# A hybrid decoder block: the causal mask added on VectorE, the latent norms' gains folded into the matrices, gates and output weights prepared in other places

## The chip, the core and the metric

The kernel runs on one core of one Trainium2 chip. A core has five engines that run side by side, each with its own queue: TensorE (PE, its weight loads PEld) for matrix products, VectorE (DVE) and ScalarE (ACT) for elementwise work, GpSimd (POOL), and SyncE (SP), which here only issues transfers. Products end in PSUM, everything else lies in SBUF. The metric is the time of one execution on the device in microseconds (us).

## What is computed

One decoder layer over 2048 tokens of width 1024, in fp32. Eight heads of attention with forget gates ("fox") and eight heads of latent attention ("mla") share an input projection; then come an output projection, a squared-ReLU MLP and a last norm. Cut to what the change touches:

```python
proj  = rmsnorm(x, attn_norm_g) @ w_in           # fq, fk, fv, f_logit, c_q, c_kv, k_rope
log_f = log_sigmoid(f_logit + b_forget)          # fox: decay, cumulated over the sequence
F     = cumsum(log_f)
c_q   = rmsnorm(proj[c_q],  q_norm_g)            # 384 wide
c_kv  = rmsnorm(proj[c_kv], kv_norm_g)           # 256 wide
k_rope = rope(proj[k_rope])
q  = c_q  @ w_uq                                 # 8 heads x (64 + 32 rotated)
kv = c_kv @ w_ukv                                # 8 heads x (64 keys + 64 values)
logits = scale * q @ k.T  (+ F_t - F_s for fox)
logits = where(key_pos <= q_pos, logits, -inf)   # causal
out = softmax(logits) @ v
mixed = concat(rmsnorm(fox, fox_out_g), rmsnorm(mla, mla_out_g))
x = x + mixed @ w_o
```

## The kernel before

Products run on fp32 values cut in two: `hi` is rounded to the format that TensorE takes at full rate, `lo` is the rest, and `mm3` (L138 to L140) makes the three products hi*hi, lo*hi, hi*lo. The cut itself is `split_ps` (from PSUM, ScalarE writes hi in L105, VectorE subtracts in L106) or `split_w` (from SBUF, L113 on GpSimd and L116 on VectorE).

The front part goes twice over 1024 tokens (pass 0 and pass 1). In each pass `latent` makes the 384 (c_q) and then the 256 + 32 + 8 columns (c_kv, rotary key, gate logit) of eight token tiles, two tiles at a time: product, copy out of PSUM, sum of squares on ScalarE (L413), the reciprocal root as six small operations on GpSimd (`rstd_pool`, L94 to L99), the scaling by root and gain on VectorE (L418), and, three steps later, the transposes (L424) and the split. `load_heads` cuts w_uq and w_ukv per group of heads. `mla_rows`, `mla_v` and `mla_qrope` multiply the latents with them and store queries, keys and values to DRAM. `rotary_keys` rotates the shared key (L496 to L499), `forget_gates` computes log sigmoid and its cumulated sum (L514 to L530, 32 operations on tiles of 128 columns, then two small products). `fox` makes the projections of the fox heads for the pass in 21 products (three of the c range, q, k and v, with seven each); while it runs, `ahead` prepares the next pass, in pass 0 the norms and transposes of the next tiles (`prep`, L350 and L355). The operand splits for fox are L589 (`split_operand`) and L609 (`fox_prep`). Work is put off by `later(n, ...)` and done by `flush`, and what is pinned (`keep_in_program_order`) stands on its engine where the program has it; the rest is placed by a scheduler.

The attention runs over units of four query tiles (a head of fox, then one of mla, two heads being one "head pair"). `score_steps` takes the keys of a query tile in chunks of up to 1024: score products into one of two buffers `ps_s` (L861), in the last chunk also the mask, as a product of a bf16 identity with a bf16 128x128 mask that is accumulated into the last 128 columns (L864); then the negated maximum on VectorE (L866), the exponential with its sum on ScalarE (L867), and a normalisation of the probabilities on GpSimd (L887) after a few 128x1 or 128x2 operations on VectorE (L875 to L884). Of 384 chunks 256 are a query tile's last. `value_steps` transposes the probabilities (L907), splits them (L105, L106), multiplies them with the values (L924, L925), and adds two halves on GpSimd after a transfer (L930, L935). All steps are laid on one list by numbers of ticks, each step at its due tick. `prepare_wo` (L950 to L952, GpSimd) multiplies the output weights by the gains and cuts them, four row blocks at a time, at two places near the end of the list.

The mask and the gain's place in the loop are these lines:

```python
if n == 0 and kb + wb == (t + 1) * P:
    nc.tensor.matmul(ps[:, i, wb - P:wb], identb, maskb, start=False, stop=False)
...
nc.vector.scalar_tensor_tensor(cn[:, b], cn[:, b], r[:, b:b + 1], gain, ALU.mult, ALU.mult)
```

## Time and profile before

| | |
|---|---|
| median of 3 runs | 2935.13 us (2934.0 to 2937.68) |
| profiled execution | 2932.08 us, its span 2930.3 us |
| PE busy | 2808.3 us, 96% |
| DVE busy | 2220.2 us, 76% |
| ACT busy | 1413.7 us, 48% |
| POOL busy | 1371.5 us, 47% |
| mean granted clock of TensorE | 0.986 |

Busy shares are of the span. The stages, in us from its start: latents of pass 0 to 112, keys and values to 150, fox of pass 0 to 263; the same for pass 1 to 350, 425 and 540; attention from 540 to 1470, whose steady part (640 to 1300) repeats every 110 us; output projection to 1640; the MLP to the end. Matmuls are pipelined, so the start-to-start step tells their cost, not the busy time of one. A wait is put down to the releaser that came last.

### The profile page before, as it was taken

To read this page: it belongs to the slowest core of one execution; us is meant where nothing else is said; L and a number is where in the kernel's file an instruction comes from. 1 tells how busy PE (TensorE), PEld (TensorE's weight loads), DVE (VectorE), ACT (ScalarE), POOL (GpSimd) and SP (SyncE) were. 2 spreads that over 40 slices of the span, in tenths; PEclk is the share of its full clock that TensorE was granted. 3 is DMA by queue.
4 is the path that set the end of the run, shared out by engine and by line. 5 is a ranking of instruction groups with operands and counts; after the bars stand their busy time and mean duration, and the time that the engine had idled before them with its cause. 6 is when DMAs were issued, how large, how long until landed. Compare 5 with 4: busy or idle time off the path is not lost. (4 is left out here: it accounts for less than half of the span.)

```text
span 2930.3 us, 40573 instructions
## 1 busy us (share of the span) xinstructions
PE 2808.3 (96%) x14634; PEld 2365.1 (81%) x14634; DVE 2220.2 (76%) x3089; ACT 1413.7 (48%) x2493; POOL 1371.5 (47%) x996
## 2 busy tenths in 40 slices
PE   8899979899999999999999899999999999999998
PEld 7789958788888888887778788888888788878886
DVE  7767486588888888888767755667666678897898
ACT  5244233487787787787533422233222433334432
POOL 2726453445545545547532355556556233453421
PEclk9999989999999999999999999999999999999999
DMA  5456434835335335332245564455445744455551
GB/s 155 160 197 190 152 133 160 236 76 121 77 93 121 76 93 121 76 93 62 69 164 208 208 208 151 143 216 223 151 158 190 269 151 148 157 212 175 199 194 58
DMA packets 262520, 442.95 MB, mean 151 GB/s; under 512 B 41712, under 2 KB 150384, under 8 KB 255600
## 3 DMA queue, kind: packets, MB, share of 16 engines
q1 hardware_dynamic: 206848, 300.75, 34.8%
q10 hardware_dynamic: 55472, 139.61, 12.4%
q8 instruction: 116, 1.90, 0.3%
q14 instruction: 84, 0.69, 0.1%
HBM read 275.54 MB, written 156.37 MB: 147 GB/s over the span
## 5 line engine op out<-in xcount | busy, mean ns | idle before, releaser
L1299 PE MATMUL mm<-big,mid 128*128 128x512 f32 x2688 | 615.9, 390 | 2.7 <-ACT big L1374 2.5
L1299 PEld LDWEIGHTS mm<-big,mid 128*128 128x128 f32 x2688 | 504.5, 188 | 112.7 <-ACT big L1374 7.2
L140 PE MATMUL mm<-big,mid 128*128 128x512 f32 x1312 | 513.9, 393 | 8.9 <-DVE mid L249 6.7
L861 PE MATMUL ps_s<-big,big 96*128 96x384 f32 (+11 forms) x1720 | 445.1, 379 | 5.3 <-ACT mid L867 5.0
L139 PE MATMUL mm<-big,big 128*128 128x512 f32 (+2 forms) x1160 | 436.5, 376 | 1.2 <-DVE big L249 1.2
L138 PE MATMUL mm<-big,big 128*128 128x512 f32 (+2 forms) x1072 | 403.5, 376 | 0.4 <-ACT big L248 0.4
L887 POOL TENSOR_SCALAR mid<-mid,rl,fac 128x768 f32<-128x768 f32 (+4 forms) x256 | 255.9, 1010 | 290.2 <-DVE rl L884 170.8
L866 DVE TENSOR_REDUCE negm<-ps_s 128x1 f32<-128x896 f32 (+7 forms) x384 | 348.2, 907 | 51.6 <-PE ps_s L861 47.5
L248 ACT ACTIVATE big<-mid 128x1024 fp32r<-128x1024 f32 (+1 forms) x222 | 218.3, 1046 | 322.4 <-PE mm L139 193.7
L255 POOL TENSOR_TENSOR mid<-mid,mid 128x1024 f32<-128x1024 f32 x88 | 241.2, 2741 | 262.2 <-DVE mid L249 112.6
L867 ACT ACTIVATE mid<-ps_s,negm 128x896 f32<-128x896 f32 (+7 forms) x384 | 332.5, 866 | 46.2 <-DVE negm L866 34.1
L907 PE MATMUL ps_t<-ident,mid 128*128 128x128 f32 x2176 | 339.8, 274 | 5.3 <-POOL mid L887 5.3
L907 PEld LDWEIGHTS ps_t<-ident,mid 128*128 128x128 f32 x2176 | 274.5, 141 | 59.1 <-POOL mid L887 5.9
L861 PEld LDWEIGHTS ps_s<-big,big 96*128 96x128 f32 (+2 forms) x1720 | 290.1, 193 | 22.2 <-ACT mid L867 9.6
L1210 POOL TENSOR_TENSOR mid<-mid,mid 128x1024 f32<-128x1024 f32 x60 | 198.8, 3340 | 232.0 <-DVE big L249 218.8
L140 PEld LDWEIGHTS mm<-big,mid 128*128 128x128 f32 x1312 | 248.1, 189 | 62.1 <-DVE mid L249 7.5
L249 DVE TENSOR_TENSOR mid<-mid,mid 128x1024 fp32r<-128x1024 f32 x112 | 193.3, 1754 | 117.4 <-ACT mid L248 83.4
L105 ACT ACTIVATE big<-ps_t 128x512 fp32r<-128x512 f32 (+3 forms) x427 | 225.0, 534 | 108.4 <-PE ps_t L907 101.0
L106 DVE TENSOR_TENSOR big<-ps_t,big 128x512 fp32r<-128x512 f32 (+3 forms) x427 | 254.2, 602 | 28.6 <-ACT big L105 25.0
L139 PEld LDWEIGHTS mm<-big,big 128*128 128x128 f32 x1160 | 220.4, 190 | 37.8 <-DVE big L249 2.0
L138 PEld LDWEIGHTS mm<-big,big 128*128 128x128 f32 x1072 | 203.8, 190 | 33.3 <-ACT big L248 1.1
L138 PE MATMUL mm<-big,mid 128*128 128x512 f32 x528 | 209.1, 397 | 12.3 <-DVE big L106 6.9
(225 smaller groups left out, 5151.9 us busy)
## 6 DMA issues: line engine op xcount, KB each, us to landing
gd<-mid ACTq DMA_DIRECT2D x109, 512.0 KB, 3.0
mid<-gd SPq DMA_DIRECT2D x109, 512.0 KB, 3.5
mid<-in_w_up SPq DMA_DIRECT2D x64, 512.0 KB, 5.2
mid<-in_w_down SPq DMA_DIRECT2D x64, 512.0 KB, 5.2
mid<-in_x SPq DMA_DIRECT2D x32, 512.0 KB, 5.8
xd<-mid ACTq DMA_DIRECT2D x28, 512.0 KB, 5.4
big<-xd SPq DMA_DIRECT2D x14, 1024.0 KB, 8.8
mid<-in_w_in SPq DMA_DIRECT2D x24, 512.0 KB, 4.0
```

Of the source, the lines that this page charges most:

```text
L105: nc.scalar.activation(hi, ps, AF.Copy)
L106: nc.vector.tensor_tensor(lo, ps, f32v(hi), ALU.subtract)
L138: nc.tensor.matmul(ps, lh, rh, start=(k == 0), stop=False)
L139: nc.tensor.matmul(ps, lh, rl, start=False, stop=False)
L140: nc.tensor.matmul(ps, ll, rh, start=False, stop=(k == nk - 1))
L255: (eng or nc.gpsimd).tensor_tensor(t, raws[a], raws[b], op)
L861: nc.tensor.matmul(ps[:, i, 0:wm], l[0:rows, qs], r[0:rows, kb:kb + wm], start=(n == 0), stop=(n == len(ops) - 1))
L866: nc.vector.tensor_reduce(negm[:, j, c:c + 1], src, AX.XY, ALU.max, negate=True)
L867: nc.scalar.activation(prob[:, 0:w].rearrange("p (b w) -> p b w", b=nb), src, AF.Exp, bias=negm[:, j, c:c + 1], accum_out=lsum[:, j, c:c + 1])
L887: nc.gpsimd.tensor_scalar(pr, pr, rl, 1.0 if nch == 1 else fac[:, j, c:c + 1], ALU.mult, ALU.mult)
L907: nc.tensor.transpose(ps[:, j * P:(j + 1) * P], prob[:, kt * P - k0:(kt + 1) * P - k0], ident)
L1299: nc.tensor.matmul(ps[:, m], l[:, k, tk(m)], r[:, :, tk(k)], start=(first and k == n == 0), stop=(k == 3 and n == 2), skip_group_check=True)
```

## The change

The mask. `maskb` becomes a tile of 1024 columns, zero but for the last 128, and the matmul of L864 goes. In a last chunk the maximum is taken by `tensor_tensor_reduce`: the scores plus the mask, times -1, written back to PSUM, with the minimum as its result; the exponential then takes a scale of -1. Other chunks keep L866.

The latent norms. The gains are multiplied into w_uq and w_ukv when these are cut (`load_heads` gets a gain for each 128 rows; GpSimd makes hi, VectorE lo, row block by row block), and the scaling by the root alone is done by ScalarE. The key rotation goes from VectorE to GpSimd.

Places. `forget_gates` is called in the second fox product of pass 1 and no longer ahead of the fox products; its two products follow after 6 steps in place of 14. In the last fox products of pass 0 a tile's transposes stand within a product. At the start, two tiles' norms stand ahead of the weight splits, which run on ScalarE and, pinned, on VectorE. The output weights are loaded and prepared one row block at a time, from the end of the first mla unit of the last head on, with the hi copy on ScalarE.

```diff
-                        if n == 0 and kb + wb == (t + 1) * P:
-                            nc.tensor.matmul(ps[:, i, wb - P:wb], identb, maskb, start=False, stop=False)
                 src = ps[:, 0:nb, 0:wb]
-                nc.vector.tensor_reduce(negm[:, j, c:c + 1], src, AX.XY, ALU.max, negate=True)
+                if c == nch - 1:
+                    nc.vector.tensor_tensor_reduce(src, src, maskb[:, 1024 - w:].rearrange("p (b w) -> p b w", b=nb),
+                                                   -1.0, -NEG, ALU.add, ALU.min, negm[:, j, c:c + 1])
+                else:
+                    nc.vector.tensor_reduce(negm[:, j, c:c + 1], src, AX.XY, ALU.max, negate=True)
                 nc.scalar.activation(prob[:, 0:w].rearrange("p (b w) -> p b w", b=nb), src, AF.Exp,
+                                     scale=-1.0 if c == nch - 1 else 1.0,
                                      bias=negm[:, j, c:c + 1], accum_out=lsum[:, j, c:c + 1])
...
-            split_w(hi, lo, raw)
+            for k in range(nk):
+                g = gain[:, k:k + 1]
+                nc.gpsimd.tensor_scalar(hi[:, k], raw[:, k], g, 1.0, ALU.mult, ALU.mult)
+                nc.vector.scalar_tensor_tensor(lo[:, k], raw[:, k], g, f32v(hi[:, k]), ALU.mult, ALU.subtract)
...
-                nc.vector.scalar_tensor_tensor(cn[:, b], cn[:, b], r[:, b:b + 1], gain, ALU.mult, ALU.mult)
+                nc.scalar.activation(cn[:, b], cn[:, b], AF.Copy, scale=r[:, b:b + 1])
...
-            nc.vector.tensor_tensor(kro, krf[:, ts4, 0:32], cos2[:, ts4], ALU.mult)
+            nc.gpsimd.tensor_tensor(kro, krf[:, ts4, 0:32], cos2[:, ts4], ALU.mult)
...
+                        if m == 1 and turns and i < 6:
+                            turns.pop(0)()
...
+            if p and c == 0 and i == 1:
+                forget_gates()
...
+                    if i == 0:
+                        prep_operands(X, 0)
+                        t0, t1 = prep(X, 0), prep(X, 1)
+                        t0()
+                        for f in splits:
+                            f()
+                        t1()
...
-            if p:
-                forget_gates()
...
+        def prepare_wo(n):
+            if n % 2 == 0:
+                wo.append((s8.get([P, 2, D]), s8.get([P, 2, D])))
+            (wh, wl), raw = (w[:, n % 2] for w in wo[-1]), wo_raw.pop(n)
+            pin(nc.gpsimd.tensor_scalar(raw, raw, go[:, n:n + 1], 1.0, ALU.mult, ALU.mult))
+            nc.scalar.activation(wh, raw, AF.Copy)
+            pin(nc.gpsimd.tensor_tensor(wl, raw, f32v(wh), ALU.subtract))
...
+                for k in range(4, 8):
+                    add(b + 14 * (k - 4), lambda k=k: load_wo(k))
+                    add(b + 14 * (k - 4) + 24, lambda k=k: prepare_wo(k))
...
+                for k in range(4):
+                    add(at + 20 * k, lambda k=k: load_wo(k))
+                    add(at + 20 * k + 24, lambda k=k: prepare_wo(k))
```

Lines of the changed kernel have other numbers: L106 becomes L105, L589 L593, L609 L613, L866 L880, L878 to L884 become L893 to L899, L887 L902, L935 L950. VectorE in a head pair of the attention, at the last chunk of one query tile and the first of the next, before:

```order
L106 TENSOR_TENSOR mid_4952<-ps_t,mid_4952 128x512
L866 TENSOR_REDUCE negm_13284<-ps_s 128x1
L106 TENSOR_TENSOR big_4951<-ps_t,big_4951 128x512 x2
L878 TENSOR_REDUCE mmin<-negm_13284 128x1
L866 TENSOR_REDUCE negm_13284<-ps_s 128x1
L106 TENSOR_TENSOR mid_4952<-ps_t,mid_4952 128x512
```

and in the changed kernel, at the same two tiles:

```order
L899 RECIPROCAL rl<-l_13172 128x1
L877 ISA ps_s,negm_13119<-ps_s,maskb 128x2x448
L877 ISA negm_13119 128x1
L105 TENSOR_TENSOR mid_4983<-ps_t,mid_4983 128x512
L893 TENSOR_REDUCE mmin<-negm_13119 128x1
L105 TENSOR_TENSOR big_4982<-ps_t,big_4982 128x512
L880 TENSOR_REDUCE negm_13119<-ps_s 128x1
```

The plain maximum of the last chunk has become a pair, the instruction on `ps_s` and one that writes only `negm`; what stands around them is placed anew but is the same in kind.

VectorE in pass 1, from the end of the forget gates to the first splits of the second fox product (L609 and L589 cut operands, L106 empties banks of PSUM), before:

```order
L528 TENSOR_TENSOR mid_3849<-mid_3849 128x128
L530 TENSOR_TENSOR mid_3849<-mid_3849 128x128
L609 TENSOR_TENSOR mid_3877<-mid_3576,mid_3876 128x1024
L106 TENSOR_TENSOR mid_3894<-mm,mid_3893 128x1024
L106 TENSOR_TENSOR big_3844<-mm,big_3844 128x128
L106 TENSOR_TENSOR mid_3925<-mm,mid_3924 128x1024
L589 TENSOR_TENSOR big_3931<-big_3531,big_3930 128x1024 x2
L609 TENSOR_TENSOR mid_3937<-mid_3578,mid_3936 128x1024
L106 TENSOR_TENSOR big_3945<-mm,big_3945 128x8x64 x2
```

and in the changed kernel, from the first keys' splits to the gates' first operations (L521 to L525):

```order
L105 TENSOR_TENSOR mid_3898<-mm,mid_3897 128x1024
L105 TENSOR_TENSOR big_3875<-mm,big_3875 128x128
L105 TENSOR_TENSOR mid_3929<-mm,mid_3928 128x1024
L105 TENSOR_TENSOR big_3949<-mm,big_3949 128x8x64
L593 TENSOR_TENSOR big_3935<-big_3562,big_3934 128x1024 x2
L521 TENSOR_TENSOR mid_4069<-krf,mid_214 128x128
L613 TENSOR_TENSOR mid_3941<-mid_3609,mid_3940 128x1024
L105 TENSOR_TENSOR big_3949<-mm,big_3949 128x8x64
L524 TENSOR_SCALAR mid_4069<-mid_4069 128x128
L105 TENSOR_TENSOR big_3969<-mm,big_3969 128x8x64 x2
L525 TENSOR_TENSOR mid_4069<-mid_4069 128x128
```

The gates' operations stand behind the two L593 and no longer ahead of all of this, and one of the 128x8x64 splits stands ahead of the two L593.

GpSimd at the first output weights, near the end of the attention (L950 gain, L951 hi, L952 lo; L887 normalises probabilities, L935 adds halves), before:

```order
L950 TENSOR_SCALAR big_15703<-big_15703,go 128x1024 x2
L951 TENSOR_SCALAR big_15705<-big_15703 128x1024 x2
L887 TENSOR_SCALAR mid_15004<-mid_15004,rl,fac_15003 128x512
L887 TENSOR_SCALAR mid_15019<-mid_15019,rl,fac_15003 128x640
L935 TENSOR_TENSOR mid_4954<-mid_4954,mid_4953 64x512
L952 TENSOR_TENSOR big_15706<-big_15703,big_15705 128x1024 x2
L887 TENSOR_SCALAR mid_15047<-mid_15047,rl,fac_15003 128x640
```

and in the changed kernel (L968 gain, L970 lo):

```order
L968 TENSOR_SCALAR mid_15095<-mid_15095,go 128x1024
L902 TENSOR_SCALAR mid_15230<-mid_15230,rl,fac_15099 128x896
L902 TENSOR_SCALAR mid_15256<-mid_15256,rl,fac_15099 128x1024
L968 TENSOR_SCALAR mid_15188<-mid_15188,go 128x1024
L970 TENSOR_TENSOR big_15224<-mid_15095,big_15223 128x1024
L902 TENSOR_SCALAR mid_15295<-mid_15295,rl,fac_15099 128x1024
L902 TENSOR_SCALAR mid_15326<-mid_15326,rl,fac_15099 128x1024
L902 TENSOR_SCALAR mid_15365<-mid_15365,rl 128x640
L970 TENSOR_TENSOR big_15224<-mid_15188,big_15223 128x1024
```

The four row blocks of 1024 columns came in twos, six instructions with three others among them; now single ones stand among the normalisations, and the hi copies have left GpSimd.

## Rows read from the trace of the kernel before

**Rows 1.** Stretches: us, busy of PE, PEld, DVE, ACT, POOL (count), PEclk, DMA share, GB/s

```profile
300.00:420.00 120.00, 105.71 (x596) 93.28 (x595) 78.82 (x114) 39.30 (x73) 62.52 (x66) 0.94 0.40 134
540.00:640.00 100.00, 89.79 (x545) 74.84 (x545) 76.27 (x171) 68.88 (x164) 41.77 (x47) 0.93 0.62 163
970.00:1080.00 110.00, 108.10 (x680) 91.62 (x679) 96.13 (x209) 87.64 (x201) 55.52 (x58) 1.00 0.41 97
```

**Rows 2.** Waits of PE, 640 to 1300 us: total us, times, longest

```profile
PE ps_t L925 <- DVE big L106: 4.6, 7, 1.4
PE ps_t L925 <- DVE mid L106: 3.2, 4, 1.4
```

**Rows 3.** Waits of PE, 100 to 150 us

```profile
PE mm L424 <- DVE mid L418: 5.2, 3, 2.0
```

**Rows 4.** Waits of PE, 350 to 430 us

```profile
PE mm L138 <- DVE big L106: 6.9, 1, 6.9
PE mm L138 <- DVE mid L106: 5.2, 3, 2.5
PE mm L424 <- DVE mid L418: 5.0, 3, 2.0
```

**Rows 5.** Line 864 on PE: count, duration min/median/max in ns, first and last start

```profile
L864 PE MATMUL ps_s<-maskb,identb x256: 219/230/330, 539.7 to 1427.6; 128*128 128x128 bf16 x128
```

**Rows 6.** Timeline of PE: start us, us, engine, line, instruction, count

```profile
984.79 1.17 PE L861 MATMUL ps_s<-big,big 96*128 96x512 f32 x4
...
986.39 0.40 PE L925 MATMUL ps_t<-big,big 128*128 128x512 f32 x1
...
988.77 1.64 PE L861 MATMUL ps_s<-big,big 96*128 96x512 f32 x6
990.25 0.40 PE L924 MATMUL ps_t<-big,big 128*128 128x512 f32 x1
```

**Rows 7.** Groups by form, VectorE, then ScalarE: busy us, mean ns, idle before

```profile
L866 DVE TENSOR_REDUCE negm<-ps_s 128x1 f32<-128x1024 f32 x64 | 78.1, 1220 | 7.4 <-PE ps_s L861 6.5
...
L418 DVE SCALAR_TENSOR_TENSOR mid<-mid,rp_r,mid 128x256 f32<-128x256 f32 x16 | 25.5, 1635 | 4.8 <-POOL rp_r L99 4.8
...
L106 DVE TENSOR_TENSOR mid<-mm,mid 128x1024 fp32r<-128x1024 f32 x8 | 9.7, 1218 | 5.9 <-ACT mid L105 5.9
...
L867 ACT ACTIVATION_READ_ACCUMULATOR mid<-ps_s,negm 128x1 f32 x384 | 77.5, 202 | 0.0
...
L413 ACT ACTIVATE junk_c<-mid 128x256 bf16<-128x256 f32 x16 | 6.6, 411 | 0.2
```

**Rows 8.** Timeline of VectorE: start us, us, instruction

```profile
1004.11 0.15 DVE L882 TENSOR_TENSOR l<-lsum,fac 128x2 f32<-128x2 f32 x1
...
1005.29 0.14 DVE L883 TENSOR_REDUCE l<-l 128x1 f32<-128x2 f32 x1
1005.40 0.15 DVE L878 TENSOR_REDUCE mmin<-negm 128x1 f32<-128x2 f32 x1
```

**Rows 9.** Timeline of VectorE, pass 0, with [idle before <- releaser]

```profile
109.30 2.94 DVE L418 SCALAR_TENSOR_TENSOR mid<-mid,rp_r,mid 128x256 f32<-128x256 f32 x2 [1.74 <-POOL rp_r L99]
112.89 5.10 DVE L418 SCALAR_TENSOR_TENSOR mid<-mid,rp_r,mid 128x256 f32<-128x256 f32 x2 [0.64 <-POOL rp_r L99]
```

**Rows 10.** Waits of PE, 0 to 60 us

```profile
PE mm L355 <- DVE mid L350: 13.9, 3, 9.4
```

**Rows 11.** Timeline of PE at the end of pass 0

```profile
257.03 1.91 PE L355 MATMUL mm<-ident,mid 128*128 128x128 f32 x16
262.10 0.36 PE L138 MATMUL mm<-mid,big 128*128 128x256 f32 x1 [3.16 <-DVE big L666]
```

**Rows 12.** Timeline of VectorE in the last head pair

```profile
1333.98 6.71 DVE L882 TENSOR_TENSOR l<-lsum,fac 128x2 f32<-128x2 f32 x1
```

**Rows 13.** Timeline of PE at the attention's start

```profile
580.90 0.47 PE L907 MATMUL ps_t<-ident,mid 128*128 128x128 f32 x1 [5.33 <-POOL mid L887]
```

**Rows 14.** The page, costliest groups: the maximum of all widths

```profile
L866 DVE TENSOR_REDUCE negm<-ps_s 128x1 f32<-128x896 f32 (+7 forms) x384 | 348.2, 907 | 51.6 <-PE ps_s L861 47.5
```

More of the change, by code (lines that the diff above doesn't have):

```diff
@@ L63, in block_kernel @@
     nc.sync.dma_start(ident, consts[:, 0:P])
-    identb = cst.tile([P, P], BF16, name="identb")
-    nc.vector.tensor_copy(identb, ident)
-    maskb = cst.tile([P, P], BF16, name="maskb")
+    maskb = cst.tile([P, 1024], BF16, name="maskb")
+    nc.vector.memset(maskb, 0.0)
     mhalf = cst.tile([P, 16], F32, name="mhalf")
@@ L380, in load_latent, with load_heads @@
                     else:
[L381 removed]
+                        splits.append(lambda hi=hi[:, k:k + 2], lo=lo[:, k:k + 2], raw=raw: (
+                            nc.scalar.activation(hi, raw, AF.Copy),
+                            pin(nc.vector.tensor_tensor(lo, raw, f32v(hi), ALU.subtract))))
             return parts
[L384 removed]
+        def load_heads(nk, src, d0, d1, h0, h1, gain):
             n = (h1 - h0) * (d1 - d0)
@@ L730, in block_kernel @@
                         nx += 1
-                    if i == 0:
-                        for f in splits:
-                            f()
-                        load_constants()
                 elif i == 2:
@@ L758, in block_kernel @@
             for i in range(8):
-                latent(X, 8 * p + i, wck, RKV, 296, g_kv, ck[i // 4], DEFER_C if i < 7 else 8)
+                latent(X, 8 * p + i, wck, RKV, 296, ck[i // 4], DEFER_C if i < 7 else 8)
                 step()
```

56 lines of the change are left out of this document (24 added, 32 removed).

## The prediction

> **What bounds the kernel now.** I read the stretches first, then the waits, then single rows. In a head pair of the attention TensorE is busy for 108.10 of 110 us, VectorE for 96.13, ScalarE for 87.64, GpSimd for 55.52, at full clock [rows 1]. So TensorE's own work is the bound there, and VectorE stands 12 us behind it. What TensorE waits for in the whole steady part, 660 us or six pairs, is mostly VectorE's split L106: 4.6 + 3.2 us, that is 1.3 us a pair [rows 2]. The picture is another in the front part: there TensorE is busy for 105.71 of 120 us and the granted clock is 0.94 [rows 1], and the reader is to see single waits of up to 7 us, each with one releaser [rows 3, 4]. The MLP and most of the output projection keep their instructions in their order on every engine, so nothing is booked there. The sum is made against the profiled execution, 2932.1 us (span 2930.3 and 1.8 us around it); it stands 3.0 us under the median of 2935.1, and these are added at the end.
>
> **The mask in the attention.** What goes: 256 bf16 matmuls, 128 columns wide, with their weight loads [rows 5]. Their busy time (0.23 us each) is no price, since matmuls overlap; the price is the step from start to start. An MLA score chunk of 1024 keys, six 512-column matmuls, takes 988.77 to 990.25, 1.48 us, without the mask, and 984.79 to 986.39, 1.60 us, with it [rows 6]: 0.12 us. 256 x 0.12 = 31 us, or 32 x 0.12 = 3.8 us a head pair. All of it is on the engine that sets the pace.
>
> What comes: for the same 256 chunks the maximum is made by one instruction that adds the mask, negates, writes the scores back and keeps the minimum, and a second small one that fetches that minimum. The trace has neither. For the first the nearest rows are the plain maximum over 1024 columns, 1.22 us, and the split's subtraction with one operand in PSUM and one in SBUF over 1024 columns, 1.218 us [rows 7]: the second operand costs nothing there, so I take the old price, with the form at half rate as the bad end (a rival, below). For the second: a 128x1 operation of VectorE behind a 128x2 one starts 0.11 us after it [rows 8], and ScalarE's fetch of an accumulator takes 0.20 [rows 7]. From below the bound is zero, as the fetch may lie in the gap that the maximum leaves now. I take 0.11 for the pair of instructions above the old one, with 0 to 0.2 as ends. That is 32 x 0.11 = 3.5 us a pair: VectorE goes to 99.6 us of about 107, from 87% to 93%.
>
> [...]
>
> The gain is not the full 31 us. VectorE's waits of 1.3 us a pair grow when it has 7 us of room where it had 14; I let them grow by 1 us. A pair comes to 110 - 3.8 + 1 = 107.2 us; eight pairs give **-22 us** (ends: -31, and 0 where VectorE sets the pace).
>
> **Scaling of the latents.** 32 scalings leave VectorE for ScalarE, without the gain vector. On VectorE a 256-column one takes 1.64 us in the mean; a ScalarE pass over 256 columns takes 0.41 [rows 7]. TensorE waits for the scaled tile three times in pass 0, 5.2 us, and three times in pass 1, 5.0 us [rows 3, 4], each at most 2.0: two scalings in turn give back 2 x 1.2 = 2.4 us. GpSimd's chain of small operations ahead of them stays, and it now gets the rotary keys' 16 operations between its steps. I take **-5 us** in pass 0 and **-4 us** in pass 1, and book **+2 us** for the rotary keys on GpSimd. The gains in the matrices cost nothing: the split of the same matrix was there before, on the same two engines, and TensorE needs it several latent tiles later; without that cover it would be 26 pairs of instructions over 256 or 512 columns, in the place of ten over 768 or 1024.
>
> **Forget gates and the start of the second fox product.** TensorE waits 6.9 us there for the first L106 [rows 4]. In VectorE's order two L589 and an L609 stand between the last ck splits and that L106, and the gate's 32 small operations ahead of all; in the changed order one L106 stands ahead of the two splits and the gates lie scattered behind. TensorE needs one bank, so most of that wait goes; what is late next is ScalarE's half of the split. **-5 us.** The other waits on L106 in that stretch, 5.2 us [rows 4], have the gates or the key rotation ahead of them; half, **-2.5 us**. At a clock of 0.94 over 120 us, 7.2 us were lost [rows 1], behind those pauses; with half of them gone I take half back, **-4 us** (ends 0 and -7).
>
> **Start, transposes, output weights.** At the start TensorE waits 13.9 us in three pieces for the first norms [rows 10]; both norms now stand ahead of the weight splits: **-2 us** (ends +3, if the first transposes come later, and -4). In the last product of pass 0 sixteen transposes came in one block and TensorE then waited 3.2 us [rows 11]; they now come eight at a time: **-2 us**. In the last head pair one 128x2 operation of VectorE took 6.71 us [rows 12] instead of 0.15 [rows 8], while GpSimd did the weights' subtractions in twos; they now come singly and the copies go to ScalarE. **-5 us** (ends 0 and -9). Queues moved past: the eight weight loads on SP now stand among the heads' loads, in a ring of buffers that the heads' own tiles share; GpSimd's instructions, one at a time now, stand among the normalisations that TensorE's transposes wait for, and ScalarE, at 87.64 of 110 us [rows 1], has room for eight copies. At the attention's start TensorE stood 5.3 us behind GpSimd's L887 [rows 13], which was behind an addition that waited for a transfer; that addition now comes two places later but its transfer stands behind two more loads. With the clock of 0.93 over those 100 us, 7 us lost [rows 1], I take **-3 us** (ends +4 and -10).
>
> Sum: -22 - 5 - 4 + 2 - 5 - 2.5 - 4 - 2 - 2 - 5 - 3 = -52.5 us, of which 30.5 lie outside the mask. 2932.1 - 52.5 + 3.0 = **2882.6 us**, I say 2882.
>
> **Rivals.** (a) VectorE becomes the attention's bound. Call d the added VectorE time a chunk. VectorE used to 98% as TensorE is now has 104 us in a pair of 106.2: the crossing is d = (104 - 96.1) / 32 = 0.25 us, and at d = 0.37 the pair is back at 110 and the mask's gain is gone: 2935.1 - 30.5 = 2905. For it: two instructions in place of one, in a chain score, maximum, exponential that holds one of only two score buffers. Against: small operations start 0.11 us apart. (b) Slower. The fused form runs at half the rate of the plain maximum: 0.907 us, the mean of 384 [rows 14], on top, with the fetch d = 1.0. VectorE then needs 96.1 + 32 = 128 us a pair, over 0.98 is 130.7, and 8 x 20.7 - 30.5 = +135 us: 3070. It decides from d = 0.48, where the loss in the attention (8 x 3.8 us) eats all else. For it: no row has a write to PSUM by VectorE or that form; against: two operands cost as one does in the rows. (c) The front doesn't do what it says: GpSimd's chain, not the scaling, sets the transposes, and the moved gates stall the fox product where they now stand. Then the mask, the weights and the transposes remain: -29 us, 2906. For it: GpSimd is the releaser ahead of the scalings in the trace; against: the scalings' own 2.94 and 5.10 us for two of 256 columns are longer than the waits [rows 9].
>
> **How the numbers follow.** Forecast (2855 to 2900) 0.53; still faster, if nearly all waits and the whole 31 us come back, 0.04; (a) with d between 0.25 and 0.45, 0.16; (c) 0.13; gains and losses cancel 0.03; (b) 0.11. A difference under 0.2%, 6 us, can't be told from none here: faster 0.86, same 0.03, slower 0.11. The range reaches from the sum with all upper ends (31 + about 51 = 82 us, 2853) to (a) at d = 0.42 and takes in (c): 2852 to 2920. (b) and a little of (a) are left out.
>
> **What would show it.** Right: a head pair of 106 to 108 us with TensorE at 98% and VectorE near 93%; the fused instruction as long as the maximum it replaces and the fetch under 0.2 us; no wait of L424 over 1 us; no wait of 6.9 us at the second fox product. Wrong: VectorE over 96% with TensorE waiting for it on most chunks; the 256 instructions longer than 1.5 times the old ones; GpSimd as the releaser of the latents' transposes; new waits where the gates stand now.

## The result and the profile after

Beside the kernel before the changed kernel took 2898.8 us in the median (four runs, 2889.4 to 2902.5) against 2934.6, a ratio of 0.9871 with a 95% interval of 0.9847 to 0.9896; timed again with the last experiments, 2893.7 against 2937.6, 0.9848 (0.9830 to 0.9867). So it is 1.3 to 1.5% faster, 36 to 44 us, where 52.5 were forecast. The profiled execution took 2889.4 us, 42.7 less than that of before.

The first fence has stretches of the changed kernel, with the columns of [rows 1]: the start of the fox products of pass 1, the attention's start, and a stretch of 110 us in its steady part.

```profile
405.00:445.00 40.00, 33.25 (x130) 25.72 (x129) 34.14 (x47) 13.27 (x14) 12.76 (x6) 0.91 0.38 131
525.00:640.00 115.00, 100.58 (x589) 87.58 (x588) 90.03 (x230) 78.63 (x186) 48.90 (x54) 0.91 0.57 145
970.00:1080.00 110.00, 109.39 (x679) 95.68 (x677) 98.00 (x251) 91.88 (x211) 57.40 (x58) 1.00 0.46 106
```

The steady part reads as forecast: VectorE is fuller, 98.0 of 110 us against 96.13, and TensorE's own share has grown from 108.10 to 109.39. In the front and at the attention's start the granted clock is still 0.91, in the mean of each stretch. Next, waits of TensorE in the changed kernel (what for, total us, times, longest), from 640 to 1270 us, as [rows 2]; from 100 to 150 (two rows), as [rows 3]; from 350 to 405 and from 405 to 445, as [rows 4]; from 250 to 270; and from 525 to 640:

```profile
PE ps_t L940 <- DVE big L105: 1.1, 4, 0.3
PE ps_t L940 <- DVE mid L105: 0.6, 2, 0.3
...
PE mm L137 <- DVE big L105: 2.7, 1, 2.7
PE mm L431 <- ACT mid L425: 0.3, 1, 0.3
...
PE mm L431 <- ACT mid L425: 0.3, 1, 0.3
...
PE mm L137 <- DVE big L105: 2.6, 1, 2.6
PE mm L542 <- DVE mid L537: 1.6, 1, 1.6
PE mm L139 <- DVE mid L613: 1.5, 1, 1.5
PE mm L137 <- ACT mid L612: 1.0, 1, 1.0
...
PE mm L137 <- DVE big L672: 7.2, 1, 7.2
...
PE ps_t L922 <- POOL mid L902: 8.3, 3, 7.0
```

The waits for VectorE in the steady part went from 7.8 us in 660 to 1.7 in 630. The waits for the scaled latents went from 5.2 and 5.0 us to 0.3 each. The wait of 6.9 us for L106 at the first matmul of the fox products of pass 1 (the prediction's second fox product) is gone, and 2.6 us for the same kind of split stand 24 matmuls later, at the next product. New or longer are 7.2 us at the end of pass 0 (3.2 before) and 8.3 us behind GpSimd at the attention's start (5.3).

To see where the time went I compare stretches of TensorE's work. All kernels here issue the same 14378 matmuls once the masks are left out, so the time from the k-th to the l-th can be set against the same time before. Each column is one profiled execution minus that of before, in us. "Steady" is 6.2 head pairs, 677.9 us before.

| stretch (matmuls) | changed | mask alone | all but mask | transposes in blocks | gates in front | latents on VectorE | start, transposes, additions | transposes, additions |
|---|---|---|---|---|---|---|---|---|
| start (0 to 100) | +2.0 | -1.4 | +3.6 | +1.2 | +3.1 | -0.7 | -0.2 | +1.3 |
| c_q, rows of pass 0 (100 to 400) | -0.2 | +1.6 | -0.8 | -0.3 | -0.5 | +2.9 | -0.3 | -0.2 |
| c_kv, keys, values (400 to 800) | -8.9 | +0.3 | -8.9 | -8.7 | -8.7 | +1.0 | -6.0 | -8.9 |
| fox of pass 0 (800 to 1200) | +2.6 | 0.0 | +3.9 | +3.9 | +3.8 | 0.0 | 0.0 | +2.0 |
| its end, start of pass 1 (1200 to 1400) | +4.2 | 0.0 | +3.9 | +0.4 | +3.9 | +3.6 | 0.0 | +1.2 |
| c_kv, keys, values of pass 1 (2000 to 2200) | -21.2 | -0.1 | -22.8 | -22.5 | -9.7 | -10.5 | -18.3 | -22.8 |
| first fox products of pass 1 (2200 to 2400) | +6.9 | 0.0 | +9.8 | +9.8 | +0.6 | +4.8 | +8.8 | +10.0 |
| attention's start (2800 to 3200) | +3.2 | +3.3 | +2.8 | +2.9 | +5.2 | +3.3 | -2.3 | -5.7 |
| steady (3200 to 7200) | -28.3 | -24.7 | +1.7 | -28.5 | -23.1 | -23.2 | -23.7 | -28.6 |
| last units (7200 to 8000) | -5.6 | +0.2 | -11.6 | -6.9 | -6.1 | -6.8 | -6.7 | -5.5 |
| output projection's start (8000 to 8200) | +7.8 | +2.6 | +4.9 | +7.7 | +8.5 | +9.7 | +8.0 | +8.0 |

The last 1422 us of the program, behind these stretches, differ by some 6 us between the columns. The stretches are read as good to 1 or 2 us, with an exception: of six profiles whose front part is that of the changed kernel (its two, all but the mask, and three runs below that change only the attention) the two stretches of pass 1 and the fox of pass 0 differ by up to 5 us, and the front part as a whole reaches from -9 to -15.

### The profile page after: what moved, and what is told of

It is laid out like the page before. It is cut to its first block, busy times and chain, and to the rows that moved or that the text cites. A ratio compares the mean times of both kernels' runs of the same rounds, so it can differ in the third digit from the quotient of the medians.

```text
span 2887.5 us, 40299 instructions
## 1 busy us (share of the span) xinstructions
PE 2782.5 (96%) x14378; PEld 2366.3 (82%) x14378; DVE 2164.2 (75%) x3313; ACT 1431.7 (50%) x2533; POOL 1378.0 (48%) x1020
## 5 line engine op out<-in xcount | busy, mean ns | idle before, releaser
L1319 PE MATMUL mm<-big,mid 128*128 128x512 f32 x2688 | 614.8, 390 | 3.1 <-ACT big L1394 2.5
L139 PE MATMUL mm<-big,mid 128*128 128x512 f32 x1312 | 513.2, 392 | 8.9 <-DVE mid L248 6.3
L872 PE MATMUL ps_s<-big,big 96*128 96x384 f32 (+11 forms) x1720 | 415.8, 366 | 5.8 <-ACT mid L881 5.7
L902 POOL TENSOR_SCALAR mid<-mid,rl,fac 128x768 f32<-128x768 f32 (+4 forms) x256 | 258.4, 1019 | 336.8 <-DVE rl L899 114.7
L247 ACT ACTIVATE big<-mid 128x1024 fp32r<-128x1024 f32 x218 | 214.9, 1050 | 316.1 <-PE mm L138 198.0
L872 PEld LDWEIGHTS ps_s<-big,big 96*128 96x128 f32 (+2 forms) x1720 | 287.6, 191 | 28.5 <-ACT mid L881 9.2
L105 DVE TENSOR_TENSOR big<-ps_t,big 128x512 fp32r<-128x512 f32 (+3 forms) x427 | 255.0, 604 | 50.0 <-ACT big L104 46.5
L877 DVE CUSTOM_DVE_ANT_0 ps_s<-ps_s,maskb 128x768 f32<-128x768 f32 (+7 forms) x256 | 228.2, 892 | 20.1 <-PE ps_s L872 17.8
L247 ACT ACTIVATE mid<-mid 128x1024 fp32r<-128x1024 f32 x112 | 114.2, 1055 | 209.6 <-POOL mid L254 85.1
```

The lines of the kernel that those rows point to most:

```text
L105: nc.vector.tensor_tensor(lo, ps, f32v(hi), ALU.subtract)
L139: nc.tensor.matmul(ps, ll, rh, start=False, stop=(k == nk - 1))
L247: nc.scalar.activation(hi, raw, AF.Copy)
L872: nc.tensor.matmul(ps[:, i, 0:wm], l[0:rows, qs], r[0:rows, kb:kb + wm], start=(n == 0), stop=(n == len(ops) - 1))
L877: nc.vector.tensor_tensor_reduce(src, src, maskb[:, 1024 - w:].rearrange("p (b w) -> p b w", b=nb), -1.0, -NEG, ALU.add, ALU.min, negm[:, ...
L902: nc.gpsimd.tensor_scalar(pr, pr, rl, 1.0 if nch == 1 else fac[:, j, c:c + 1], ALU.mult, ALU.mult)
```

## The experiments

**The mask alone, and all but the mask.** The first is the kernel before with the mask's edit and nothing else, the second the changed kernel with the mask back on TensorE:

```diff
-                        if n == 0 and kb + wb == (t + 1) * P:
-                            nc.tensor.matmul(ps[:, i, wb - P:wb], identb, maskb, start=False, stop=False)
...
+                if c == nch - 1:
+                    nc.vector.tensor_tensor_reduce(src, src, maskb[:, 1024 - w:]...)
+                else:
+                    nc.vector.tensor_reduce(negm[:, j, c:c + 1], src, AX.XY, ALU.max, negate=True)
```

> The kernel before with the mask edit alone. Theory A (TensorE sets the attention's pace and gets back the start-to-start cost of 256 mask matmuls; the fetch of the minimum lies in a gap that was there): 28 to 31 us less than before, all of it between the attention's start and its end, front part and MLP unchanged. Rival B (the mask gives less, since VectorE fills up, and a good part of the measured gain is from the front part): 12 to 20 us less. Under A the wait of TensorE for VectorE in the steady part is no longer than the 7.8 us of before, under B it is longer.

> The changed kernel with the mask back on TensorE: everything of the change but the mask. Theory A: 5 to 12 us less than before (the changed kernel's median is 36 us less, and some 29 of it are the mask's). Rival B: 16 to 24 us less. By the prediction's own terms the parts outside the mask were to bring 30.5 us; if they bring that, the mask brought next to nothing.

Measured: the mask alone 2914.0 us against 2931.3, ratio 0.9928 (0.9906 to 0.9949), 17 us; all but the mask 2916.7, 0.9945 (0.9928 to 0.9961), 15 us. Together they make 32 of the 36 to 44 us of the changed kernel. By the totals theory A fails, which wanted 28 to 31 us, and rival B has the number, 12 to 20, but not the reason: the waits for VectorE in the steady part shrink, where B has them grow, and the front part gains nothing. By the stretches A holds in the steady part: it is 24.7 us shorter, and all but the mask leaves it as it was (+1.7). The waits of the kernel with the mask alone, 640 to 1290 us:

```profile
PE ps_t L928 <- DVE big L105: 1.0, 4, 0.2
PE ps_t L928 <- DVE mid L105: 0.5, 2, 0.2
```

What is missing of the 28 to 31 us is at the edges of the attention: +3.3 at its start, where TensorE waits 7.2 us at once for GpSimd, which waits for a transfer (8.22 us in that profile, 8.13 in the changed kernel), +2.6 at the output projection, and nothing gained in the last units. There single operations of other engines end the waits, in the kernel with the mask alone VectorE's L886 the longest of the last units (4.9 us) and L1146 one of 2.6 us at the output projection. Over the attention and the output projection's start together the mask is worth 19 us in the kernel with the mask alone, and 21 us when the changed kernel is set against all but the mask.

The instruction itself, in the changed kernel, by form (busy us, mean ns) and in the timeline (start us, us):

```profile
L877 DVE CUSTOM_DVE_ANT_0 ps_s<-ps_s,maskb 128x1024 f32<-128x1024 f32 x48 | 59.0, 1228 | 2.6 <-PE ps_s L872 2.0
...
L877 DVE DVE_READ_ACCUMULATOR2_ANT negm<- 128x1 f32 x256 | 36.2, 141 | 0.0
...
L880 DVE TENSOR_REDUCE negm<-ps_s 128x1 f32<-128x1024 f32 x16 | 19.5, 1220 | 2.3 <-PE ps_s L872 2.3
...
992.02 0.70 DVE L877 CUSTOM_DVE_ANT_0 ps_s<-ps_s,maskb 128x512 f32<-128x512 f32 x1 [0.21 <-PE ps_s L872]
992.64 0.14 DVE L877 DVE_READ_ACCUMULATOR2_ANT negm<- 128x1 f32 x1
992.64 1.44 DVE L105 TENSOR_TENSOR big<-ps_t,big 128x512 fp32r<-128x512 f32 x2
```

The fused form takes 1.228 us over 1024 columns where the plain maximum of this profile takes 1.220. Its fetch has a busy time of 0.14 us, but the next instruction starts at 992.64 too, as the fetch does, so these rows give it no time of its own. My term for it was 0.11 us a chunk, with zero as the lower end; it is the lower end.

**How much room VectorE has.** One more instruction behind each masked maximum, which nothing waits for; its length is 128 or 384 columns:

```diff
                     nc.vector.tensor_tensor_reduce(src, src, maskb[:, 1024 - w:]...)
+                    nc.vector.tensor_reduce(maskb[:, 0:1], maskb[:, 0:384], AX.X, ALU.max)
```

> The changed kernel with one more VectorE instruction behind each of the 256 masked maxima: a maximum over 128 zeros of the mask, nothing waits for it. It adds about 0.2 us of VectorE time a chunk. Theory A (VectorE has room): within 10 us of the changed kernel, a head pair under 107.5 us. Rival B (VectorE is at its limit already): 32 x 0.2 = 6.4 us a pair, some 50 us more than the changed kernel.

> As the run with the short extra instruction, with 384 columns: about 0.47 us of VectorE time a chunk, 15 us a head pair on top of the changed kernel's 98. The prediction's crossing lies at 0.25 us a chunk and it has the pair back at 110 us with 0.37. By that: a pair of (98.3 + 15) / 0.98 = 115.6 us, the attention 70 to 80 us longer than in the changed kernel and the whole some 40 us slower than before. Rival C (the busy times of VectorE overlap by their fill, so that its room is larger than they say): a pair under 111 us and the whole no slower than before.

Measured: 2912.2 us (0.9929, 0.9913 to 0.9946) and 2918.1 (0.9950, 0.9931 to 0.9970). Both are slower than the changed kernel and faster than before. The same 110 us of the steady part in the one and in the other, and the long one's instruction and the waits of TensorE with it (640 to 1270 us):

```profile
970.00:1080.00 110.00, 108.42 (x664) 94.58 (x663) 103.16 (x278) 89.41 (x206) 55.94 (x58) 1.00 0.43 98
```

```profile
970.00:1080.00 110.00, 107.19 (x649) 92.14 (x649) 106.93 (x274) 87.59 (x201) 55.54 (x58) 1.00 0.42 97
```

```profile
990.43 0.54 DVE L879 TENSOR_REDUCE maskb<-maskb 128x1 bf16<-128x384 bf16 x1
990.89 0.14 DVE L899 TENSOR_REDUCE l<-l 128x1 f32<-128x2 f32 x1
```

```profile
PE ps_t L941 <- DVE l L899: 3.8, 6, 0.6
PE ps_t L941 <- DVE big L105: 3.7, 11, 0.6
PE ps_t L941 <- DVE mid L105: 2.0, 6, 0.6
```

From 990.43 to 990.89 the long instruction costs 0.46 us. The steady part gives a pair of 105.4 us in the changed kernel (649.6 / 6.16), 107.4 with the short one, 110.0 with the long one. So a pair is back at the time of before with 0.46 us a chunk; the prediction put this at 0.37, and its 98% of use is about what the row of the long one shows (107.2 busy for TensorE, 106.9 for VectorE, of 110). Each of these two kernels has an order of its own on TensorE in the steady part. Two other orders differ by 5 us there (below), so some of the 12 us of the short one can be its order, and from where on VectorE sets the pace is known no better than somewhere under 0.46 us. For the short one theory A's bound on a pair, 107.5 us, just holds and its 10 us on the whole do not (13 us by the medians, 17 to 24 by the ratios); rival B's 6.4 us a pair and 50 us are far off. For the long one rival C holds: no slower than before, and not the 40 us more that the prediction's own sum gave. The busy times of VectorE overlap by some 0.08 us from one instruction to the next (990.43 and 0.54 make 990.97, and the next starts at 990.89), and so they overstate what it is short of.

**Latents on VectorE again.** The changed kernel with L418 and the unscaled matrices back:

```diff
-                nc.scalar.activation(cn[:, b], cn[:, b], AF.Copy, scale=r[:, b:b + 1])
+                nc.vector.scalar_tensor_tensor(cn[:, b], cn[:, b], r[:, b:b + 1], gain, ALU.mult, ALU.mult)
```

> The changed kernel with the latents' scaling by root and gain on VectorE again and the matrices without gains. By the prediction's term the scaling brought 5 us in pass 0 and 4 us in pass 1: the stretches of the c_kv latents get 4 to 5 us longer each than in the changed kernel, with TensorE waiting for the scaled tile again, three times each. Rival (GpSimd's chain ahead sets it): under 1 us in each.

Measured: 2913.9 us, 0.9936 (0.9919 to 0.9952). Counted from the kernel before it is 16 to 24 us slower than the changed kernel, 5 of them in the steady part, which has another order (below). TensorE's waits there, 100 to 150 us and 350 to 405 us:

```profile
PE mm L137 <- DVE big L105: 6.8, 1, 6.8
PE mm L426 <- DVE mid L420: 6.0, 4, 2.0
...
PE mm L426 <- DVE mid L420: 5.2, 3, 2.0
```

In the changed kernel ScalarE's two scalings take 0.91 us where VectorE's took 2.94 and 5.10 [rows 9]:

```profile
108.57 0.91 ACT L425 ACTIVATE mid<-mid,rp_r 128x256 f32<-128x256 f32 x2 [1.74 <-POOL rp_r L98]
...
113.08 0.91 ACT L425 ACTIVATE mid<-mid,rp_r 128x256 f32<-128x256 f32 x2 [1.51 <-POOL rp_r L98]
```

The waits for the scaled tile are back, 6.0 and 5.2 us, so GpSimd's chain does not set them and rival (c) falls. More comes back than these: 6.8 us for L105 in pass 0, where the changed kernel has 2.7 in the waits shown above. Over the front part (0 to 2400) this kernel is 16 us longer than the changed one, which the table gives as the sum of its differences, and 11 to 16 longer than the six profiles with that front part. What stands ahead of that split on VectorE in this run:

```profile
134.65 3.55 DVE L420 SCALAR_TENSOR_TENSOR mid<-mid,rp_r,mid 128x256 f32<-128x256 f32 x2
138.12 6.64 DVE L588 TENSOR_TENSOR big<-big,big 128x1024 fp32r<-128x1024 f32 x2
```

The scalings did not only delay their own transposes, they stood ahead of the splits on the same queue. But more of that wait is under the two operand splits behind them (L588; L593 in the changed kernel), 6.64 us for instructions that take 1.22 each elsewhere; the next experiment comes back to them.

**Gates in front again.**

```diff
-            if p and c == 0 and i == 1:
-                forget_gates()
...
+            if p:
+                forget_gates()
             fox_prep(0)
```

> The changed kernel with the forget gates where they were, ahead of the fox products of pass 1. In the changed kernel the stretch before these products is 21 us shorter than before and the one behind them 7 us longer. Theory A (the gates made both): 14 us of the two come back, so that this kernel is some 10 to 14 us slower than the changed one. Rival D (the first is from the scaling on ScalarE and from the rotated keys on GpSimd, the second from the gates): the first stretch stays 15 us or more shorter, the 7 us go, and the kernel is faster than the changed one by some 5 us.

Measured: 2903.9 us, 0.9897 (0.9879 to 0.9915), where the changed kernel has 0.9871 and 0.9848. That is 8 to 14 us slower, theory A's number, but 5 us of it are the steady part with its other order. The stretch ahead of the fox products is 11.5 us longer than in the changed kernel, the one behind 6.3 us shorter. So the place of the gates is worth 5 us net there, 1 to 5 against the six profiles: more than half of what is won ahead is paid back behind, and theory A's 14 us were too many. Rival D's order of sizes fails too, since the latents (10.7 us by the run above) and the gates (11.5) each make half of the 21 us.

A long wait for VectorE's split is back, but not the one that the prediction named. Below are TensorE's rows: the named wait in the kernel before, at the first matmul of the fox products; then a matmul 50 places ahead of it, among the keys and values, with the gates in front, with the latents on VectorE, and in the first and the second profile of the changed kernel.

```profile
425.79 0.79 PE L138 MATMUL mm<-big,mid 128*128 128x512 f32 x1 [6.88 <-DVE big L106]
...
404.49 1.30 PE L137 MATMUL mm<-mid,mid 128*128 128x512 f32 x2 [8.90 <-DVE big L105]
...
410.33 1.30 PE L137 MATMUL mm<-mid,mid 128*128 128x512 f32 x2 [6.81 <-DVE big L105]
...
390.46 0.73 PE L137 MATMUL mm<-mid,mid 128*128 128x512 f32 x2 [1.02 <-ACT mid L104]
...
393.32 1.30 PE L137 MATMUL mm<-mid,mid 128*128 128x512 f32 x2 [4.81 <-DVE big L105]
```

The run with the latents on VectorE has the gates in their new place and waits 6.81 us there, and one program, the changed kernel, waits 1.02 or 4.81. So this wait is not the gates' alone. VectorE's two operand splits right ahead of it and GpSimd's instruction beside them, in the first profile of the changed kernel and in the second:

```profile
386.73 2.36 DVE L593 TENSOR_TENSOR big<-big,big 128x1024 fp32r<-128x1024 f32 x2 [0.34 <-ACT big L592]
387.97 3.35 POOL L568 TENSOR_TENSOR big<-big,big 128x1024 f32<-128x1024 f32 x1
...
385.82 6.75 DVE L593 TENSOR_TENSOR big<-big,big 128x1024 fp32r<-128x1024 f32 x2 [0.34 <-ACT big L592]
385.82 2.39 POOL L568 TENSOR_TENSOR big<-big,big 128x1024 f32<-128x1024 f32 x1
```

The same two splits take 2.36 us where GpSimd starts behind them and 6.75 where it starts with them. In five profiles (before, the changed kernel's two, latents, gates) there are 80 of these splits: the 50 that no GpSimd instruction of more than 1 us overlaps take 1.21 to 1.23 us each, and of the other 30, 22 take 1.5 to 3.5. No run tests this by itself, but such stretched splits stand ahead of each of the long waits above, that of the kernel before too (its two L589 take 4.52 us).

The gates two fox products later, on top of the run with start, transposes and additions of the next paragraphs:

```diff
-            if p and c == 0 and i == 1:
+            if p and c == 0 and i == 3:
                 forget_gates()
```

> The run with start, transposes and additions as before, with the forget gates two fox products later. In all kernels with the gates in the second product the stretch behind the first fox products of pass 1 is 7 to 10 us longer than before. Theory A (the gates' 32 operations on VectorE hold up the operand splits of the next products): it comes down to 3 us or less, and the kernel gets 4 to 6 us faster than that run. Rival (the fox products start earlier than their operands come, and the gates do not matter): no difference over 2 us.

Measured: 2885.0 us, 0.9828 (0.9809 to 0.9847), against 0.9849 (0.9833 to 0.9864) with the gates in the second product; the intervals overlap. The stretch is +7.0 us where it was +8.8, not the 3 or less of theory A, but the front part as a whole is 5 us shorter, more than the rival's 2 and no more than like front parts differ by: neither is borne out. Nor does this run take the gates out of the stretch, since TensorE waits 3.7 us there for their sums (L535; 1.6 us with the gates in the second product):

```profile
PE mm L540 <- DVE mid L535: 3.7, 1, 3.7
PE mm L137 <- DVE big L105: 2.3, 1, 2.3
```

Two columns of the table say more. With the gates in front and with the latents on VectorE the stretch ahead is about as long (-9.7 and -10.5 us); the stretch behind is +0.6 with the gates in front and +4.8 with the gates within it, which points to some 4 us for the gates themselves; these are single profiles of a stretch that differs by up to 5.

**Transposes in blocks again.**

```diff
                         mm3(pv[:, m], ...)
-                        if m == 1 and turns and i < 6:
-                            turns.pop(0)()
```

> The changed kernel with the transposes of the next tiles behind a product again, not within it (the last fox products of pass 0). In the changed kernel TensorE waits 7.2 us at the end of that product where it waited 3.2 before. Theory A (the new place of the transposes makes that wait): the stretch from the last fox products of pass 0 to the first latents of pass 1 is 4 us shorter than in the changed kernel. Rival (the wait is from the additions behind the products, which come later for another reason): it stays, within 1 us.

Measured: 2889.0 us, 0.9848 (0.9827 to 0.9868), no faster than the changed kernel's second ratio. The stretch at the end of pass 0 goes from +4.2 to +0.4, as theory A has it. The front part as a whole is -16.6 us where the changed kernel has -14.9 and, in its second profile, -12.7. Two rows of VectorE in the changed kernel and two in this one say why; L352 is the norm of a coming tile, and TensorE waits for the addition, L672 in the one and L670 in the other:

```profile
256.88 3.35 DVE L352 SCALAR_TENSOR_TENSOR mid<-mid,rp_rx,mid 128x1024 f32<-128x1024 f32 x1
260.15 1.21 DVE L672 TENSOR_TENSOR big<-big,mm 128x1024 f32<-128x1024 f32 x1
```

```profile
257.17 1.21 DVE L670 TENSOR_TENSOR big<-big,mm 128x1024 f32<-128x1024 f32 x1
258.30 2.96 DVE L352 SCALAR_TENSOR_TENSOR mid<-mid,rp_rx,mid 128x1024 f32<-128x1024 f32 x1
```

With the transposes within the product, the norm of the second tile goes ahead of the addition on VectorE, and it takes 3.35 us there. I had counted the transposes' own block of 1.9 us and not what their earlier place lets through on another engine.

**Start, transposes and additions; transposes and additions.** In the first the start is as before too; in both the additions of the first two units on GpSimd (L950) come later:

```diff
-            add(b + STORE, lambda u=unit: u["v"][1]())
+            add(b + (56 if n == 0 else 40 if n == 1 else STORE), lambda u=unit: u["v"][1]())
```

> The changed kernel with the start and the transposes as before, and with the first two units' additions on GpSimd put off by 30 and 14 ticks, so that the normalisations ahead of the transposes do not stand behind a transfer. The start gives 2 to 3 us, the transposes 4, and the wait of 7 us at the attention's start goes, with the lower clock behind it: 10 to 15 us less than the changed kernel in all. Rival (the wait moves to the next instruction that waits for the same transfer): under 6 us less.

> The changed kernel with the transposes in blocks again and with the first two units' additions on GpSimd put off by 30 and 14 ticks; the start as in the change. Its steady attention has the same order on TensorE as the changed kernel's (28 us shorter than before there), where the run with the start undone too had another one (24 us shorter). Theory A: the 4 us of the transposes, the 5 us of the attention's start and the 28 us add up: 45 to 50 us less than before, some 5 us less than either of those two runs. Rival (the steady part's length does not go with the order): as the run with the start undone, 45 us or less.

Measured: 2888.1 us, 0.9849 (0.9833 to 0.9864), and 2881.6 us, 0.9807 (0.9793 to 0.9822). The first misses its theory, 10 to 15 us less than the changed kernel: by the ratios it is 0 to 6. The second is faster than before by 56 us, more than the 45 to 50 of its theory, and beside the changed kernel on the same chip (2893.7) by 12. The row of GpSimd before and in the changed kernel, and TensorE's wait for it in the second of these runs from 525 to 640 us:

```profile
578.73 1.25 POOL L935 TENSOR_TENSOR mid<-mid,mid 64x512 f32<-64x512 f32 x1 [6.53 <-DMA mid<-mid]
...
569.50 1.25 POOL L950 TENSOR_TENSOR mid<-mid,mid 64x512 f32<-64x512 f32 x1 [8.13 <-DMA mid<-mid]
```

```profile
PE ps_t L920 <- POOL mid L900: 0.8, 1, 0.8
```

The addition waited 8.13 us for its transfer with the normalisations behind it; put off, TensorE's wait for GpSimd goes from 8.3 to 0.8 us, and the attention's start from +3.2 to -2.3 and -5.7. The two loads that stand ahead of the transfer in the changed kernel explain little of it: the addition starts 14.9 us after the transfer is issued (at 554.64), and 13.5 us before the change, when the transfer was issued (at 565.19) ahead of the same two loads. The kernel with the mask alone, which moves no load, has the same wait, 8.22 us, and loses the same 3 us there. The start undone gives 2 us in its stretch, and 3 us are lost in the keys and values of pass 0 behind it (-6.0 against -8.9). But the run with it undone is not the faster one: its steady part is -23.7, that of the other -28.6. Compared matmul by matmul, the changed kernel, the runs with the transposes in blocks, with transposes and additions, and with the weights in halves have the same order on TensorE all through the steady part; the mask alone and the four runs with gates, latents or start undone or gates later, with -23 to -25 us, share another one. The scheduler chose between them, in four of these runs from edits hundreds of microseconds ahead. The 5 us go with the order in all ten profiles; whether the order on TensorE makes them, or something on another engine that goes with it, was not tested.

**The changed kernel again.**

> The changed kernel itself, beside the others on one chip, for the comparison and for a second profile: its first four times lie 13 us apart. Where the longer ones spend it, if this profile is of one: the granted clock, spread over all stretches (as the clocks of 0.983 to 0.986 go), or one stretch, in which then a wait stands that the first profile does not have.

Measured: 2893.7 us, 0.9848 (0.9830 to 0.9867). Its profile (2892.4 us) lies 3 us above the first: 1 us each at the start, in the keys and values and the first fox products of pass 1, and at the attention's start. Its wait of 4.81 us for VectorE (above) stands where the first profile has 1.02, and the 2.6 us of the first at the second fox product are not there. Its eight times, the first four and these, span 15 us; these four span 9, as those of before beside them do. What makes the longer ones is open, as no profile is of one of them.

**Weights in halves again.**

```diff
-        def prepare_wo(n):
+        def prepare_wo(half):
...
+                    nc.gpsimd.tensor_scalar(wh[:, k], raw[:, k], 1.0, 1.0, ALU.mult, ALU.mult)
```

> The changed kernel with the output weights prepared in two blocks of four again, all on GpSimd. Theory A (the single blocks bring what the last head pair lost, the prediction's 5 us, in the run with the mask alone 4 us longer than before there, in the changed kernel 5.5 us shorter): this kernel is 5 to 10 us slower. Rival (the gain is given back at the output projection's first tiles, which in the changed kernel take 8 us more than before): within 3 us of the changed kernel.

Measured: 2890.2 us, 0.9838 (0.9824 to 0.9853), within the interval of the changed kernel beside it. Theory A fails, and the rival holds nearly: by the medians this kernel is 3.4 us faster. The last units are 8.6 us shorter than before with the old weights too (5.6 in the changed kernel), so that gain is not the weights', and the output projection's start is +2.9 us where the changed kernel has +7.8. The longest wait of TensorE at the start of the output projection in the changed kernel (1440 to 1470 us), and the same in this one (from the waits of 1270 to 1480):

```profile
PE mm L1058 <- DVE mid L1163: 4.9, 1, 4.9
```

```profile
PE mm L1053 <- DVE mid L1158: 2.7, 1, 2.7
```

The new place of the weights saves nothing: the two stretches together pay 8 us for it, of which the medians, not clear of their noise, show 3.

## Why the forecast held, and where its terms did not

The sign, the place of most of the gain and the range held; the sum was 9 to 17 us too large. That it is no farther off is in part luck: the latents brought 2 to 7 us more than booked, the gates 6 to 10 less, and four small terms, booked with 12 us together, brought nothing or cost something. Against its own steps:

| term | forecast | measured, and by which run |
|---|---|---|
| mask, attention | -22 | -19 (mask alone) and -21 (changed kernel against all but the mask) from the attention's to the output projection's start; -25 and -30 of it in the steady part |
| scaling of the latents | -9 | -11 to -16 in the front part (latents undone) |
| rotary keys on GpSimd | +2 | undone in no run |
| gates, fox products of pass 1, clock | -11.5 | -1 to -5 in the two stretches (gates undone) |
| start | -2 | +2 in its stretch, -3 in the one behind (undone) |
| transposes | -2 | +4 in their stretch (undone) |
| output weights | -5 | +8 in the last units and the output projection's start, +3 in the medians (undone) |
| attention's start | -3 | +3, with the mask alone too; -2 to -6 with the additions put off |

The mask. The price of 0.12 us a matmul fits, and so does its place. The step that failed is "they grow by 1 us a pair": the waits on VectorE shrank, from 1.3 us a pair to 0.3. I had argued from VectorE's share, put at 93% (the row of the changed kernel has 98.0 of 110 us, 89%). That the new order has fewer places where a split stands behind single operations is my reading and was not counted. Measured, a pair went from 110.0 to 105.4 us, 4.6 less, where 3.8 of the masks and 1.0 of waits make 4.8; with the mask alone and the other order the waits shrank as much and the pair by 4.0, so this sum is not closed. That -22 comes close for the whole is chance: of it 17 lie in the steady part, which gave 25 to 30, and 5 at the attention's edges, where 6 to 9 were lost. The upper end of my term, -31 for eight pairs, assumed that all eight are alike; the first and last units are not.

The fetch, 0.11 us, was mis-sized and is next to nothing; its lower bound was right. The rival of a form at half rate fell at the first row, 1.228 us. For rival (a), the room of VectorE was put at 0.25 us a chunk and the old time at 0.37; the extra instruction shows the old time at 0.46.

The latents. "Two scalings in turn give back 2 x 1.2" priced the instruction and its wait and left out the queue. Undone, the waits for the scaled tile make 11 us, and the rest is splits of VectorE that came later behind the scalings and the stretched operand splits. The term that I took as -9 is -11 to -16; the rotary keys stand on GpSimd in both kernels of this comparison, so their +2 is in neither.

The gates. The wait of 6.9 us at the first fox product is gone, as the order said, and 2.6 us stand at the second. What failed is the step "what is late next is ScalarE's half of the split", with which the term ended: the stretch behind lost 5 to 10 us that had no term. Its rows before and in the changed kernel, from matmul 2200 to 2400 and with the columns of [rows 1]:

```profile
436.44:481.12 44.68, 44.68 (x201) 37.08 (x200) 31.61 (x28) 16.95 (x18) 10.34 (x4) 1.00 0.54 182
414.65:466.25 51.60, 47.41 (x202) 37.90 (x201) 38.41 (x51) 20.93 (x23) 11.04 (x4) 0.97 0.48 166
```

Of the 6.9 us, 4.1 are the waits shown above: 1.6 for the gates' own sums (L537) and 2.5 for operands of the next products (L612, L613), which were not yet ready for products that now start earlier. The other 2.7 are TensorE's busy time, 47.41 us where it was 44.68, at a granted clock of 0.97 where it was 1.00; 3% of 51.6 us makes 1.5 of them, an estimate from these two rows, and what makes the rest was not shown. So the sign of being wrong that I had named, new waits where the gates stand now, showed in part.

Two small terms had the wrong sign in their own stretch and a third at the attention's start. The transposes and the weights were argued from the wait before, without asking which instruction the new order puts ahead of the one that TensorE waits for. For the attention's start I named the addition two places later and its transfer behind two more loads, and booked a gain from the first; the addition waits 8.13 us for the transfer where it waited 6.53, TensorE stands 8.3 us behind it where it stood 5.3, and as the mask alone has much the same, neither movement is shown to be the cause. The term of the start is +2 and -3 in two stretches and so no clear gain or loss.

## What to carry over

A piece of work that leaves the bound engine pays its start-to-start cost (here 0.12 us for a matmul with a busy time of 0.23), which is found by setting one stretch with it against a like one without; whether the engine that takes it over has room is asked by giving that engine a little more still, as its busy times here overlapped by some 0.08 us from one instruction to the next and so overstated what it was short of. Ask of an instruction that waits what stands behind it on its queue, and not only who waits for its result: behind GpSimd's addition, held for 8.13 us, stood the normalisations and then TensorE, for 7.0 us in its longest wait. A wait that comes back is the same wait only if it stands at the same matmul, and two profiles of one program differed there by 4 us here (1.02 and 4.81). And where a scheduler places the work, an edit moves stretches it does not touch: attribute by undoing one part at a time and comparing stretches, not totals.

## What was not expected of the hardware

A VectorE instruction that reads scores in PSUM and a mask in SBUF, writes the scores back and keeps a minimum took as long as the maximum alone (1.228 and 1.220 us for 1024 columns), and the fetch of the minimum, 0.14 us by its row, delayed the next instruction by nothing that the timeline shows. A VectorE subtraction over 128 x 1024 values in SBUF (L588, L589, L593) took 1.21 to 1.23 us with no GpSimd instruction of more than 1 us beside it and 1.5 to 3.5 us in 22 of the 30 cases with one; in one profile of the changed kernel GpSimd's L568 started 1.24 us behind the first of two such splits, in another with it. On GpSimd a transfer of 64 x 512 values was waited for 8.13 us, 14.9 us after its issue, with the normalisations and then TensorE behind the wait; 30 ticks more (some 12 us, an estimate from a head pair of 110 us and 272 ticks) brought TensorE's wait for GpSimd from 8.3 to 0.8 us.
